# The causal mask of an attention kernel moved from TensorE into the row-maximum instruction, and 128-column products paired

## The chip, the cores and the metric

The kernel runs on one core of one Trainium2 chip. A core has a matrix engine (TensorE, PE in the profile; its weight loads are shown apart as PEld), a vector engine (VectorE, DVE), an engine for functions of one operand (ScalarE, ACT), a general one (GpSimd, POOL) and DMA queues that several engines issue (SP, ACT, POOL). Each engine works through its own list of instructions in order; semaphores order the engines among each other. Operands lie in SBUF, and matmul results in PSUM. Columns stand for the elements along the free dimension, of which each of the 128 partitions has a row.

The metric is the device time of one execution in microseconds (us). Lower is better.

## What is computed

One layer of a decoder, for 512 tokens of width 1024, in float32. The input is normalised, one projection feeds a gated linear attention with four heads and a multi-head latent attention (MLA) with eight heads, both are projected back and merged by gates, and after a residual and a second normalisation comes a squared-ReLU MLP of width 4096. The part that the change touches is the causal softmax of the MLA:

```python
for blk in range(seq // Q_BLOCK):                     # four blocks of 128 queries
    q0, q1 = blk * Q_BLOCK, (blk + 1) * Q_BLOCK
    s = (jnp.einsum('bhqd,bhkd->bhqk', q_nope[:, :, q0:q1], k_nope[:, :, :q1])
         + jnp.einsum('bhqr,bkr->bhqk', q_rope[:, :, q0:q1], k_rope[:, :q1]))
    s = s.astype(jnp.float32) * scale
    mask = (q0 + jnp.arange(Q_BLOCK))[:, None] >= jnp.arange(q1)[None, :]
    p = jax.nn.softmax(jnp.where(mask, s, -jnp.inf), axis=-1).astype(v.dtype)
    outs.append(jnp.einsum('bhqk,bhkv->bhqv', p, v[:, :, :q1]))
```

A block of queries reads the keys up to its own end, so the blocks have 128, 256, 384 and 512 keys, and only the last 128 of each need a mask.

## The kernel before

Matmuls run in a float32 format of reduced precision. To keep float32 accuracy, each operand is split into a high part (rounded, by ScalarE) and a low part (the difference, by VectorE), and a product is the sum of three matmuls: high by high, high by low, low by high. For the weights `pump` does this split (lines 189 and 190) some steps ahead of their use; for activations `split` does (lines 111, 112, 114 and 115). The generic projections are `gemm_fm` (matmuls on lines 245 to 247) and `gemm_tm` (279 to 281).

Work beside the main stream of projections is written as generators. A projection calls `tick` after each of its steps, which lets the first few waiting generators go on to their next `yield`. This gives the order in which instructions are handed to the framework; the framework is asked to plan each engine's order itself (`schedule_with_timeline_sim=True`), so an engine's list follows that plan. `tc.issue_after` puts single instructions behind another one on their engine. Within an engine the order is fixed when the program is built.

The MLA works on pairs of heads. `mla_pair` (line 953) projects queries, keys and values of two heads and starts two generators `mla_head` (line 973), the second some steps after the first. A head goes through four tiles of 128 queries. For tile i with n = 128 (i + 1) keys, a PSUM bank from the pool `px` (four banks, shared with other work) takes:

- three matmuls for the part without positions (lines 984 to 986): high queries by high keys, high by low, low by high;
- two matmuls for the rotary part (lines 987 and 988). Its stationary operand holds the high and the low part of the query on its 128 rows together;
- one matmul of an identity by a mask in bfloat16 (line 989), 0 where a key may be seen and -1e30 where not, onto the last 128 columns.

VectorE then takes the negative of the row maximum from PSUM (991), ScalarE the exponential with that as its bias, from PSUM to SBUF, and the row sum at the same time (994). VectorE inverts the sum (995) and scales the row (996). Once a head's four tiles are there, PE transposes them (1008), they are split, and three matmuls for each block of keys multiply them by the values (1027 to 1029). Then follows the output projection `y_mla`, which `omT` feeds.

Tiles 0 and 2 of a head share one SBUF buffer, `P02`: columns 0 to 127 for tile 0 and 128 to 511 for tile 2. The others come from the pool `B` with 22 buffers.

The constants come with a packed array. `cb` (lines 471 to 474) holds gains, biases, the mask (`neg`) and the rotary frequencies; `identb` (470) and `negb` (491) are its bfloat16 copies that the mask matmul reads. ScalarE's queue issues the DMAs of these constants.

Of the kernel before, what the change touches and what calls it, by code (L numbers as in the profile page):

```python
# [22 lines left out]
NT = T // P  # L23
NK = D // P
LN_EPS = 1e-5
RMS_EPS = 1e-6
GH = 4
# [21 lines left out]
PACK_B = 3 + 2 + NK + GH + 2 * NK + 2 * NK + P + 32  # L49
# [3 lines left out]
def tile_hybrid_block(ctx: ExitStack, tc: tile.TileContext, I, out, dbg=None):  # L53
    nc = tc.nc
    dbg = dbg or {}
    consts = ctx.enter_context(tc.tile_pool(name="consts", bufs=1))
# [9 lines left out]
    def nm(s):  # L66
        uid[0] += 1
        return f"{s}_{uid[0]}"
# [8 lines left out]
    def B(shape, dt=F32, n="b"):  # L77
        return pb.tile(shape, dt, tag="B", name=nm(n))
# [11 lines left out]
    def PX(shape=(P, T), dt=F32, n="px"):  # L90
        return px.tile(list(shape), dt, tag="px", name=nm(n))
# [4 lines left out]
    act = nc.scalar.activation  # L96
# [4 lines left out]
    mm = nc.tensor.matmul  # L101
# [27 lines left out]
    ident = ca[:, 0:P]  # L129
# [2 lines left out]
    mhalf = consts.tile([P, 8], F32, name="mhalf")  # L132
    nc.vector.memset(mhalf, -0.5)
    identr = consts.tile([P, P], F32R, name="identr")
    identb = consts.tile([P, P], BF, name="identb")
    negb = consts.tile([P, P], BF, name="negb")


    stream = []
# [327 lines left out]


    act(identr, ident, AF.Copy)
    act(identb, ident, AF.Copy)  # L470
    cb = consts.tile([P, PACK_B], F32, name="cb")
    nc.scalar.dma_start(cb, I["c_pack_b"])
    cut = np.cumsum([0, 3, 2, NK, GH, 2 * NK, NK, NK, P, 32]).tolist()
    qag, kvg, glg, bga, bgt, ln1g, ln1b, neg, invf = [cb[:, cut[i]:cut[i + 1]] for i in range(9)]
    posi = consts.tile([P, NT], I32, name="posi")
    nc.scalar.dma_start(posi, I["positions"].rearrange("(t p) -> p t", p=P))
    lmask = consts.tile([P, len(LEVELS), 64], U8, name="lmask")
# [1 line left out]
    nc.scalar.dma_start(lmi, I["c_lmask"])  # L479
    wa2 = B([80, T], F32, "wa2")  # L480
    nc.gpsimd.memset(wa2, 0.0)
    for i in range(3):
        nc.scalar.dma_start(wa2[32 * i:32 * i + 16, :], I["w_gla_a2"])
    hbg = consts.tile([P, 2 * NK], F32, name="hbg")
# [3 lines left out]
    def prep():  # L488
        with tc.issue_after(last_in.ins):
            vts(hbg, bgt, 0.5, None, op0=ALU.mult)  # L490
            nc.vector.tensor_copy(negb, neg)
            nc.vector.tensor_copy(lmask, lmi)
        posf = consts.tile([P, NT], F32, name="posf")
        with tc.issue_after(last_in.ins):
            nc.vector.tensor_copy(posf, posi)
        ang = B([P, NT, 32], F32, "ang")
        for tt in range(NT):
            vts(ang[:, tt, :], invf, posf[:, tt:tt + 1], None, op0=ALU.mult)
        yield
        angs = []  # L500
        for sh in (0.0, 0.25):
            kq = B([P, NT, 32], F32, "kq")
            vts(kq, ang, 1.0 / (2.0 * math.pi), sh, op0=ALU.mult, op1=ALU.add)
            vts(kq, kq, MAGIC, None, op0=ALU.add)
            vts(kq, kq, MAGIC, None, op0=ALU.subtract)
            r = B([P, NT, 32], F32, "rr")
            stt(r, kq, -TWO_PI_1, ang, op0=ALU.mult, op1=ALU.add)
            stt(r, kq, -TWO_PI_2, r, op0=ALU.mult, op1=ALU.add)
            stt(r, kq, -TWO_PI_3, r, op0=ALU.mult, op1=ALU.add)
            vts(r, r, sh * 2.0 * math.pi, PI_F, op0=ALU.add, op1=ALU.min)  # L510
            vts(r, r, -PI_F, None, op0=ALU.max)
            angs.append(r)
            yield
        act(sn2[:, :, 32:], angs[0], AF.Sin)
        act(cs2[:, :, :32], angs[1], AF.Sin)
        nc.vector.tensor_copy(cs2[:, :, 32:], cs2[:, :, :32])
        vts(sn2[:, :, :32], sn2[:, :, 32:], -1.0, None, op0=ALU.mult)
        yield
# [403 lines left out]
    scale = HQ ** -0.5  # L922
# [50 lines left out]
    def mla_head(h, hl, qn, kn, vt):  # L973
        for _ in range((0 if h == MH - 1 else STAG) * hl):
            yield
        KK, qs = KKs[0], QS[h]
        Ps = []
        P02 = B([P, T], F32, "P02")
        for i in range(NT):
            n = P * (i + 1)  # L980
            c = slice(i * P, (i + 1) * P)
            p = PX()
            o = p[:, :n]
            mm(o, qn[:, 0, c], kn[:, 0, :n], start=True, stop=False)
            mm(o, qn[:, 0, c], kn[:, 1, :n], start=False, stop=False)
            mm(o, qn[:, 1, c], kn[:, 0, :n], start=False, stop=False)
            mm(o, qs[:, c], KK[:, 0, :n], start=False, stop=False)
            mm(o, qs[:, c], KK[:, 1, :n], start=False, stop=False)
            mm(p[:, c], identb, negb, start=False, stop=True)
            mx = S([P, 1], F32, "mx")  # L990
            nc.vector.tensor_reduce(mx, p[:, :n], axis=AX.X, op=ALU.max, negate=True)
            Pm = P02[:, :P] if i == 0 else P02[:, P:] if i == 2 else B([P, T], F32, "Pm")
            sme = S([P, 1], F32, "sme")
            act(Pm[:, :n], p[:, :n], AF.Exp, bias=mx, accum_out=sme)
            nc.vector.reciprocal(sme, sme)
            vts(Pm[:, :n], Pm[:, :n], sme, None, op0=ALU.mult)
            Ps.append(Pm)
            if i != 0:
                yield

        PT = [A([P, 2, T], F32R, "PT0"), A([P, 2, T], F32R, "PT1"), B([P, 2, 256], F32R, "PT2")]
        plan_t = ([(i, 0, i) for i in range(4)], [(i - 1, 1, i) for i in range(1, 4)] + [(3, 3, 3)],
                  [(i - 2, 2, i) for i in range(2, 4)])
        for b, (pl, pt) in enumerate(zip(plan_t, PT)):
            n = len(pl) * P
            p = PX()
            for cc, j, i in pl:
                nc.tensor.transpose(p[:, cc * P:(cc + 1) * P], Ps[i][:, j * P:(j + 1) * P], ident)
            split(p[:, :n], pt[:, 0, :], pt[:, 1, :])
            if b != 1:  # L1010
                yield
        PT0, PT1, PT2 = PT
        while vt[NT - 1] is None:
            yield
        o = PX()
        for j in range(NT):
            c = slice(hl * P, (hl + 1) * P)
            vh, vl = vt[j][:, 0, c], vt[j][:, 1, c]
            if j == 0:
                ph, pl, od = PT0[:, 0, :], PT0[:, 1, :], o  # L1020
            elif j == 1:
                ph, pl, od = PT1[:, 0, :384], PT1[:, 1, :384], o[:, 128:]
            elif j == 2:
                ph, pl, od = PT2[:, 0, :], PT2[:, 1, :], o[:, 256:]
            else:
                ph, pl, od = PT1[:, 0, 384:], PT1[:, 1, 384:], o[:, 384:]
            mm(od, vh, ph, start=j == 0, stop=False)
            mm(od, vh, pl, start=False, stop=False)
            mm(od, vl, ph, start=False, stop=j == NT - 1)
        yield  # L1030
        om = A([P, 2, T], F32R, "omT")
        st["om"] = split(o, om[:, 0, :], om[:, 1, :])
        omT[h] = om
# [613 lines left out]
```

## Time and profile before

| | before |
|---|---|
| median of three runs | 887.67 us (886.94 to 888.92) |
| profiled execution, first to last instruction (its span) | 884.5 us |
| what lies around the span, against the median | 3.2 us |
| TensorE busy | 868.1 us, 98% |
| weight loads busy | 760.3 us, 86% |
| VectorE busy | 638.4 us, 72% |
| ScalarE busy | 473.6 us, 54% |
| first and last start of a score matmul of line 984 | 344.6 and 453.5 us |

The profile gives one figure for its execution, the span; the time of that very execution as the runs measure it is not listed, so its distance to the median is the best that can be said.

How to read the rows that follow. A row of the timeline has the start (us), the duration (us), the engine, the line of the kernel, the operation, what it writes `<-` what it reads by the program's names, and the shape of the output and of one input; `128*128` ahead of a matmul's shape is the part of the array in use; `x2` means that two instructions in a row are shown as one; a bracket at the end shows how long the engine was idle before, and what ended that. A row of the groups has, after the count, the busy time (us), the mean duration of one instruction (ns), then the idle time before them (us) and what ended it. Matmuls overlap each other, so the distance between their starts tells what one of them costs. The chain that ended last follows the run back from its last instruction, at each step to what released it.

### The profile page before, as it was taken

What the parts mean: (1) busy time and instruction counts of PE and PEld (TensorE: products, weight loads), DVE (VectorE), ACT (ScalarE), POOL (GpSimd) and SP (SyncE); (2) the same over time, 40 slices, a digit from 0 to 9 for tenths busy, and PEclk for the clock granted to TensorE, in tenths of its full rate; (3) what the DMA queues carried; (4) which work ended last, traced back from release to release, by engine and by line L of the source; (5) the groups of instructions that cost most, each with busy time, mean ns of one, the idle gap of its engine ahead of it and who ended that gap; (6) DMA issues with size and microseconds to landing.
All of it is one profiled execution on the core that took longest, in us unless ns stands there. A gap on an engine that the chain in (4) does not pass through costs nothing.

```text
span 884.5 us, 13143 instructions
## 1 busy us (share of the span) xinstructions
PE 868.1 (98%) x4916; PEld 760.3 (86%) x4916; DVE 638.4 (72%) x1019; ACT 473.6 (54%) x834; POOL 185.7 (21%) x200
## 2 busy tenths in 40 slices
PE   6999999999999999999999999999999999999996
PEld 5988888889999988888888888988888888889985
DVE  7859879959665646646866797887557646788865
ACT  6556676556475534435654414566357546656820
POOL 1314457854201010100000003004400520141000
PEclk9999999999999999999999999999999999999999
DMA  7995936795737423112307528006941990399312
GB/s 247 283 221 152 324 110 162 229 215 168 215 87 194 144 78 102 54 54 63 99 19 268 191 72 285 1 1 167 291 113 29 261 254 28 85 232 231 121 61 81
DMA packets 91023, 132.50 MB, mean 150 GB/s; under 512 B 8992, under 2 KB 54432, under 8 KB 90960
## 3 DMA queue, kind: packets, MB, share of 16 engines
q1 hardware_dynamic: 70672, 92.36, 32.5%
q0 software_dynamic: 18368, 35.66, 18.8%
q10 hardware_dynamic: 1920, 3.66, 1.2%
q8 instruction: 38, 0.62, 0.3%
q14 instruction: 25, 0.20, 0.1%
HBM read 110.15 MB, written 8.91 MB: 135 GB/s over the span
## 4 chain that ended last, share of the span: by engine, by line
PE 98%; DMA 1%; ACT 0%; DVE 0%; POOLq 0%; issue 0%; DVEq 0%; ACTq 0%
PE mm L247 11%; PE mm L245 11%; PE mm L246 11%; PE mm L279 6%; PE mm L280 6%; PE mm L281 6%; PE mm L1172 4%; PE mm L1174 4%; PE mm L1173 4%; PE px L1460 2%; PE px L1458 2%; PE px L1459 2%; PE px L849 2%; PE mm L1460 2%; PE mm L1458 2%; PE mm L1459 2%
## 5 line engine op out<-in xcount | busy, mean ns | idle before, releaser
L190 DVE TENSOR_TENSOR wlo<-wraw,whi 128x1024 fp32r<-128x1024 f32 (+1 forms) x90 | 100.1, 1112 | 91.4 <-ACT whi L189 86.6
L189 ACT ACTIVATE whi<-wraw 128x1024 fp32r<-128x1024 f32 (+1 forms) x90 | 85.5, 950 | 81.3 <-PE mm L246 34.7
L246 PE MATMUL mm<-h,whi 128*128 128x512 f32 x224 | 87.2, 389 | 0.0
L245 PE MATMUL mm<-h,whi 128*128 128x512 f32 x224 | 87.1, 390 | 0.0
L247 PE MATMUL mm<-h,wlo 128*128 128x512 f32 x224 | 83.2, 390 | 0.0
L190 DVE TENSOR_TENSOR wlo<-wq,whi 128x1024 fp32r<-128x1024 f32 x44 | 54.5, 1239 | 30.0 <-ACT whi L189 30.0
L1477 POOL DMA_DIRECT2D res<-ev x42 | 37.4, 1000 | 180.7 <-ACT ev L1475 151.5
L189 ACT ACTIVATE whi<-wq 128x1024 fp32r<-128x1024 f32 x44 | 46.5, 1057 | 27.1 <-PE mm L1173 19.0
L1173 PE MATMUL mm<-sh,whi 128*128 128x256 f32 x176 | 49.9, 283 | 0.0
L1172 PE MATMUL mm<-sh,whi 128*128 128x256 f32 x176 | 49.9, 283 | 0.0
L1174 PE MATMUL mm<-sh,wlo 128*128 128x256 f32 x176 | 49.8, 283 | 0.0
L247 PEld LDWEIGHTS mm<-h,wlo 128*128 128x128 f32 x224 | 42.0, 188 | 9.1 <-DVE wlo L190 0.4
L246 PEld LDWEIGHTS mm<-h,whi 128*128 128x128 f32 x224 | 42.0, 188 | 8.8
L245 PEld LDWEIGHTS mm<-h,whi 128*128 128x128 f32 x224 | 42.0, 188 | 8.6
L189 ACT ACTIVATE xh<-wraw 128x1024 fp32r<-128x1024 f32 (+1 forms) x28 | 27.5, 987 | 28.0 <-PE mm L281 15.8
L429 POOL TENSOR_TENSOR mv<-mv,mhalf 128x1 f32<-128x1 f32 x4 | 3.3, 837 | 170.4 <-DVE mv L428 170.4
L190 DVE TENSOR_TENSOR xl<-wraw,xh 128x1024 fp32r<-128x1024 f32 (+1 forms) x28 | 31.3, 1129 | 8.7 <-ACT xh L189 8.7
L793 ACT ACTIVATE E<-rp 128x256 f32<-128x256 f32 x64 | 25.8, 418 | 20.5 <-POOL rp L788 13.7
L1520 ACT ACTIVATE relu<-mm 128x512 f32<-128x512 f32 x24 | 14.1, 596 | 42.0 <-PE mm L247 42.0
L788 POOL TENSOR_TENSOR rp<-rp 128x256 f32<-128x256 f32 x32 | 33.0, 1030 | 9.8 <-ACT q L818 6.1
L787 POOL TENSOR_TENSOR rp<-rp 128x256 f32<-128x256 f32 x32 | 29.6, 926 | 25.3 <-ACT E L793 18.1
L1174 PEld LDWEIGHTS mm<-sh,wlo 128*128 128x128 f32 x176 | 33.8, 192 | 0.0
(472 smaller groups left out, 2821.4 us busy)
## 6 DMA issues: line engine op xcount, KB each, us to landing
wraw<-in_w_ff_dram SPq DMA_DIRECT2D x36, 512.0 KB, 4.8
wraw<-in_w_in_dram SPq DMA_DIRECT2D x30, 512.0 KB, 4.7
wq<-in_w_ff_dram POOLq DMA_DIRECT2D x26, 512.0 KB, 9.4
res<-ev POOLq DMA_DIRECT2D x42, 256.0 KB, 9.4
wq<-in_w_in_dram SPq DMA_DIRECT2D x20, 512.0 KB, 6.6
wq<-in_w_in_dram POOLq DMA_DIRECT2D x18, 512.0 KB, 9.9
hsd<-hs SPq DMA_DIRECT2D x16, 256.0 KB, 3.8
xr<-hsd SPq DMA_DIRECT2D x16, 256.0 KB, 3.7
```

The costliest lines, as they stand in the source:

```text
L189: st["ins"] = act(hi[:, :nk, :n], raw[:, :nk, :n], AF.Copy)
L190: st["lo"] = vtt(lo[:, :nk, :n], raw[:, :nk, :n], f(hi[:, :nk, :n]), op=ALU.subtract)
L245: mm(o, hi[:, c], xh, start=first, stop=False)
L246: mm(o, hi[:, c], xl, start=False, stop=False)
L247: mm(o, lo[:, c], xh, start=False, stop=last)
L279: mm(o, xh, hi[:, :n], start=opens, stop=False, skip_group_check=share)
L280: mm(o, xh, lo[:, :n], start=False, stop=False, skip_group_check=share)
L281: mm(o, xl, hi[:, :n], start=False, stop=last, skip_group_check=share)
L1172: mm(oa, hi[:, k, c], xh, start=opens and k == 0 and a == 0, stop=False, skip_group_check=True)
L1173: mm(oa, hi[:, k, c], xl, start=False, stop=False, skip_group_check=True)
L1174: mm(oa, lo[:, k, c], xh, start=False, stop=k == 3, skip_group_check=True)
L1477: nc.gpsimd.dma_start(res[tt + t][:, j * T:(j + 1) * T], e, accum_op=ALU.add)
```

## The change

The mask matmul goes, and with it the two bfloat16 constants. The mask becomes a float32 tile `masks` of 512 columns, zeros in the first 384 (a memset on GpSimd) and the mask itself in the last 128, so that its last n columns are the mask of a tile with n keys. The packed constants are loaded in three DMAs in place of one, the middle one straight into `masks`.

The row maximum is taken by one instruction on VectorE with two operands, scores and mask. It writes minus their sum to SBUF, and the minimum of that over the row, which is minus the maximum, to `mx`. The exponential then reads this SBUF row with a scale of -1, in place, and no longer PSUM.

The first tile of a head, with 128 keys, gets its five products in three matmuls: the products with the high and the low part of the keys stand side by side as one matmul of 256 columns (two runs of 128 in SBUF), and a further reduction on VectorE adds both halves, from PSUM into the part of `P02` that tile 2 uses later.

```diff
-    identb = consts.tile([P, P], BF, name="identb")
-    negb = consts.tile([P, P], BF, name="negb")
+    masks = consts.tile([P, T], F32, name="masks")
...
-    act(identb, ident, AF.Copy)
-    cb = consts.tile([P, PACK_B], F32, name="cb")
-    nc.scalar.dma_start(cb, I["c_pack_b"])
+    cb = consts.tile([P, PACK_B - P], F32, name="cb")
+    n0 = PACK_B - P - 32
+    for dst, c0, n in ((cb[:, :n0], 0, n0), (masks[:, T - P:], n0, P), (cb[:, n0:], n0 + P, 32)):
+        nc.scalar.dma_start(dst, I["c_pack_b"][:, c0:c0 + n])
...
     nc.gpsimd.memset(wa2, 0.0)
+    nc.gpsimd.memset(masks[:, :T - P], 0.0)
...
-            nc.vector.tensor_copy(negb, neg)
...
-            mm(o, qn[:, 0, c], kn[:, 0, :n], start=True, stop=False)
-            mm(o, qn[:, 0, c], kn[:, 1, :n], start=False, stop=False)
-            mm(o, qn[:, 1, c], kn[:, 0, :n], start=False, stop=False)
-            mm(o, qs[:, c], KK[:, 0, :n], start=False, stop=False)
-            mm(o, qs[:, c], KK[:, 1, :n], start=False, stop=False)
-            mm(p[:, c], identb, negb, start=False, stop=True)
+            if i == 0:
+                w = p[:, :2 * P].rearrange("p (two k) -> p two k", two=2)
+                mm(w, qn[:, 0, c], kn[:, :, :P], start=True, stop=False, skip_group_check=True)
+                mm(o, qn[:, 1, c], kn[:, 0, :P], start=False, stop=False, skip_group_check=True)
+                mm(w, qs[:, c], KK[:, :, :P], start=False, stop=True, skip_group_check=True)
+                s0 = P02[:, P:2 * P]
+                nc.vector.tensor_reduce(s0, p[:, :2 * P].rearrange("p (two k) -> p k two", two=2), axis=AX.X, op=ALU.add)
+                o = s0
+            else:
+                mm(o, qn[:, 0, c], kn[:, 0, :n], start=True, stop=False)
+                mm(o, qn[:, 0, c], kn[:, 1, :n], start=False, stop=False)
+                mm(o, qn[:, 1, c], kn[:, 0, :n], start=False, stop=False)
+                mm(o, qs[:, c], KK[:, 0, :n], start=False, stop=False)
+                mm(o, qs[:, c], KK[:, 1, :n], start=False, stop=True)
+            Pm = P02[:, :P] if i == 0 else P02[:, P:] if i == 2 else B([P, T], F32, "Pm")
             mx = S([P, 1], F32, "mx")
-            nc.vector.tensor_reduce(mx, p[:, :n], axis=AX.X, op=ALU.max, negate=True)
-            Pm = P02[:, :P] if i == 0 else P02[:, P:] if i == 2 else B([P, T], F32, "Pm")
+            nc.vector.tensor_tensor_reduce(Pm[:, :n], o, masks[:, T - n:], scale=-1.0, scalar=3e38,
+                                           op0=ALU.add, op1=ALU.min, accum_out=mx)
             sme = S([P, 1], F32, "sme")
-            act(Pm[:, :n], p[:, :n], AF.Exp, bias=mx, accum_out=sme)
+            act(Pm[:, :n], Pm[:, :n], AF.Exp, scale=-1.0, bias=mx, accum_out=sme)
```

More of the change, by code (lines that the diff above doesn't have):

```diff
@@ L469, in tile_hybrid_block @@
     act(identr, ident, AF.Copy)
-    act(identb, ident, AF.Copy)
-    cb = consts.tile([P, PACK_B], F32, name="cb")
-    nc.scalar.dma_start(cb, I["c_pack_b"])
-    cut = np.cumsum([0, 3, 2, NK, GH, 2 * NK, NK, NK, P, 32]).tolist()
-    qag, kvg, glg, bga, bgt, ln1g, ln1b, neg, invf = [cb[:, cut[i]:cut[i + 1]] for i in range(9)]
+    cb = consts.tile([P, PACK_B - P], F32, name="cb")
+    n0 = PACK_B - P - 32
+    for dst, c0, n in ((cb[:, :n0], 0, n0), (masks[:, T - P:], n0, P), (cb[:, n0:], n0 + P, 32)):
+        nc.scalar.dma_start(dst, I["c_pack_b"][:, c0:c0 + n])
+    cut = np.cumsum([0, 3, 2, NK, GH, 2 * NK, NK, NK, 32]).tolist()
+    qag, kvg, glg, bga, bgt, ln1g, ln1b, invf = [cb[:, cut[i]:cut[i + 1]] for i in range(8)]
     posi = consts.tile([P, NT], I32, name="posi")
```

## The prediction

> **What bounds the kernel now.** I read the page first: the span, the busy times and the chain of work that ended last.
>
> ```profile
> span 884.5 us, 13143 instructions
> PE 868.1 (98%) x4916; PEld 760.3 (86%) x4916; DVE 638.4 (72%) x1019; ACT 473.6 (54%) x834; POOL 185.7 (21%) x200
> PE 98%; DMA 1%; ACT 0%; DVE 0%; POOLq 0%; issue 0%; DVEq 0%; ACTq 0%
> ```
>
> TensorE is busy 98% of the span and makes 98% of the chain. So a matmul taken out is worth its time, provided that nothing else becomes late. The place that decides is the attention stage, from about 345 to 460 us. The second view is the busy time by stretch; columns: busy PE, weight loads (PEld), VectorE (DVE), ScalarE (ACT), GpSimd (POOL), with instruction counts, then clock and DMA.
>
> ```profile
> 345.00:460.00 115.00, 115.00 (x685) 98.91 (x684) 76.48 (x187) 58.59 (x144) 3.04 (x4) 1.00 0.20 61
> ...
> 420.00:440.00 20.00, 20.00 (x126) 17.46 (x125) 17.30 (x41) 13.67 (x34) 0.00 (x0) 1.00 0.31 99
> 440.00:460.00 20.00, 20.00 (x119) 16.85 (x118) 11.97 (x35) 8.87 (x26) 0.00 (x0) 1.00 0.04 14
> ```
>
> In these 115 us PE has no gap, the clock granted is 1.00, and VectorE, which gets the new work, is busy 76.48 us, so 38.5 are free. The tight stretch is 420 to 440 us: 17.30 of 20.
>
> **Term 1, the mask matmuls.** A busy PE hides overlap (a matmul's duration is longer than its distance to the next), so prices are distances between starts. Third view: the timeline of PE and its weight loads at the first head.
>
> ```profile
> 345.63 0.27 PE L987 MATMUL px<-KK,QS 128*128 128x128 f32 x1
> 345.68 0.19 PEld L988 LDWEIGHTS px<-KK,QS 128*128 128x128 f32 x1
> 345.74 0.28 PE L988 MATMUL px<-KK,QS 128*128 128x128 f32 x1
> 345.85 0.10 PEld L989 LDWEIGHTS <-identb 128*128 128x128 bf16 x1
> 345.85 0.23 PE L989 MATMUL px<-negb,identb 128*128 128x128 bf16 x1
> 345.86 0.20 PEld L985 LDWEIGHTS px<-qn,qn 128*128 128x128 f32 x1
> 345.89 0.37 PE L985 MATMUL px<-qn,qn 128*128 128x256 f32 x1
> 346.10 0.28 PE L986 MATMUL px<-qn,qn 128*128 128x256 f32 x1
> 346.22 0.28 PE L987 MATMUL px<-KK,QS 128*128 128x256 f32 x1
> ...
> 346.46 0.23 PE L989 MATMUL px<-negb,identb 128*128 128x128 bf16 x1
> 346.50 0.42 PE L985 MATMUL px<-qn,qn 128*128 128x384 f32 x1
> 346.75 0.33 PE L986 MATMUL px<-qn,qn 128*128 128x384 f32 x1
> 346.92 0.34 PE L987 MATMUL px<-KK,QS 128*128 128x384 f32 x1
> ```
>
> From L987 to L988 (128 columns) is 0.11 us; between two of 256 columns 0.12 (346.10 to 346.22); of 384 columns 0.17 (346.75 to 346.92). The mask's own step is 0.04 (345.85 to 345.89), but the matmul behind it needs 0.21 in place of 0.12, since its weight load only began at 345.86, behind the mask's. So a mask costs 0.25 - 0.12 = 0.13 in the first place and 0.29 - 0.17 = 0.12 in the second. I take 0.12. There are eight heads of four query tiles:
>
> ```profile
> L989 PE MATMUL px<-negb,identb 128*128 128x128 bf16 x32 | 7.3, 230 | 0.0
> L988 PE MATMUL px<-KK,QS 128*128 128x128 f32 x8 | 2.2, 274 | 0.0
> ```
>
> 32 x 0.12 = 3.84 us off PE. Lower bound: only the step itself goes and the wait for the next weights stays, 32 x 0.04 = 1.3.
>
> **Term 2, the first tile's pairs.** Five matmuls of 128 columns (5 x 0.11 = 0.55) become 256 + 128 + 256 columns, 0.12 + 0.11 + 0.12 = 0.35. That is 0.20 for each of the x8 first tiles, 1.6 us. The moving operand now comes in two runs of 128 columns, a form that this trace does not show; if each run cost a matmul of its own, nothing would be gained. Bounds 0 to 1.6; I take 1.6, since the nearest row is the 256-column one. A loss would need a run to cost more than a whole matmul of the same columns.
>
> PE in all: 3.84 + 1.6 = 5.4 us less.
>
> **What VectorE gets.** The fourth view is the groups by shape, VectorE and then ScalarE.
>
> ```profile
> L991 DVE TENSOR_REDUCE mx<-px 128x1 f32<-128x512 f32 x8 | 5.5, 688 | 3.5 <-PE px L989 3.2
> L991 DVE TENSOR_REDUCE mx<-px 128x1 f32<-128x256 f32 x8 | 3.4, 421 | 1.2 <-PE px L989 1.2
> L991 DVE TENSOR_REDUCE mx<-px 128x1 f32<-128x128 f32 x8 | 2.3, 286 | 1.2 <-PE px L989 1.1
> L112 DVE TENSOR_TENSOR PT<-px,PT 128x512 fp32r<-128x512 f32 x12 | 7.8, 684 | 2.6 <-ACT PT L111 2.6
> L112 DVE TENSOR_TENSOR mv<-mm,mv 128x256 fp32r<-128x256 f32 x16 | 6.4, 415 | 0.0
> L995 DVE RECIPROCAL sme<-sme 128x1 f32<-128x1 f32 x32 | 5.1, 160 | 3.6 <-ACT Pm L994 3.0
> ...
> L994 ACT ACTIVATION_READ_ACCUMULATOR Pm<-px,mx 128x1 f32 x16 | 3.1, 193 | 0.0
> L111 ACT ACTIVATE mv<-mm 128x256 fp32r<-128x256 f32 x16 | 5.6, 380 | 2.5 <-DVE mv L112 2.5
> L189 ACT ACTIVATE whi<-wraw 128x256 fp32r<-128x256 f32 x4 | 1.7, 418 | 5.7 <-PE mm L281 4.4 <-PE mm L246 0.7 <-ACT omT L111 0.6
> ```
>
> The fused add-and-minimum isn't in the trace. Its nearest rows are the two-operand instruction from PSUM and SBUF (415 ns at 256 columns, 684 at 512) against the reduction that it replaces (421, 688): no difference. The minimum may need an instruction of its own to be read out, as the sum on ScalarE does (193 ns). Bounds 0 to 0.19; I take 0.16, the [P,1] instruction of the same engine. The first tile gets a further reduction of 256 columns, 0.42. Per head 4 x 0.16 + 0.42 = 1.06 us, for eight 8.5. Lower end 0.42 per head (readout free; a gain is excluded, since as many columns are passed as before). Upper end: the fused instruction takes two cycles for a column. One column is (688 - 286) / 384 = 1.05 ns, so a head's 1280 columns add 1.34, with 4 x 0.19 and 0.42 in all 2.5 per head, 20 us. Even 20 fit into the 38.5 free. In 420 to 440 us lie two score tiles of each width, two heads' worth (the same view for that stretch alone):
>
> ```profile
> L991 DVE TENSOR_REDUCE mx<-px 128x1 f32<-128x512 f32 x2 | 1.4, 688 | 0.6 <-PE px L989 0.6
> ```
>
> There VectorE comes to 17.30 + 2.1 = 19.4 of 20 as I take it, and to 17.30 + 5.0 = 22.3 at the upper end, 2.3 over.
>
> [...]
>
> **Why that isn't on the path.** The chain of a tile (scores, maximum, exponential, scaling, transposes) grows by the readout, and by 0.04 where the exponential reads SBUF in place of PSUM (418 - 380 ns). Behind it PE's queue, which is in order, holds the transposes and then projections. Fifth view: the timeline where scaled tiles meet the transposes that may read them, at the first head and at the last two.
>
> ```profile
> 352.00 0.49 DVE L996 TENSOR_SCALAR Pm<-Pm,sme 128x512 f32<-128x512 f32 x1
> ...
> 354.65 0.27 PE L1008 MATMUL px<-ca,Pm 128*128 128x128 f32 x1
> ...
> 456.00 0.48 DVE L996 TENSOR_SCALAR Pm<-Pm,sme 128x512 f32<-128x512 f32 x1
> 456.75 0.49 DVE L996 TENSOR_SCALAR Pm<-Pm,sme 128x512 f32<-128x512 f32 x1
> ...
> 457.93 0.27 PE L1008 MATMUL px<-ca,Pm 128*128 128x128 f32 x1
> ```
>
> At the first head the last scaled tile is ready at 352.49 and read at 354.65: 2.2 us to spare. At the end it is 0.7 (457.93 - 457.24) to 1.5 (from 456.48), by which of the two is read first. My 1.06 per head fits the first and about fills the second. The fused instruction also waits for its SBUF target, which the exponential did later; behind it on VectorE stand the low halves of the weights, for which PE waits. The PSUM bank comes free before the exponential in place of after it, but PE has no gap to win there. I put all this at 0.
>
> **The start.** ScalarE's queue issues two more DMAs and drops a copy, GpSimd gets a memset of 384 columns.
>
> ```profile
> 1.18 0.45 ACTq L472 DMA_DIRECT2D cb<-in_c_pack_b_dram  x1
> 7.01 1.24 ACT L433 ACTIVATE x<-x,nmr,mvin 128x1024 f32<-128x1024 f32 x1 [2.37 <-DVE nmr L432]
> 8.60 0.52 POOL L481 MEMSET wa<- 80x512 f32 x1
> 21.35 1.44 POOL L429 TENSOR_TENSOR mvin<-mvin,mhalf 128x1 f32<-128x1 f32 x1 [12.23 <-DVE mvin L428]
> ```
>
> 2 x 0.45 goes into the 2.37 us that ScalarE waits before L433, and some 0.5 of memset into GpSimd's 12.23. If that cover went, 0.9 would be lost. The bytes of cb are the same. I take 0.
>
> **Sum.** 884.5 - 5.4 = 879.1 us of span. The median of the three runs is 887.67, 3.2 above the profiled span; the same difference gives 882.3 us, 0.6% faster. 0.2% of 887.67, 1.8 us, is about what a measurement of this kernel can tell from no change.
>
> **The rivals.**
> *The pairs gain nothing* (term 2 at 0): 887.67 - 3.84 = 883.8. For it: the form is new here. Against it: no row shows a price for a moving operand that isn't in one run.
>
> *A short matmul costs by its columns.* From 256 to 384 columns the distance grows by 0.05, so 128 columns would be 0.06. Then a mask is worth 32 x 0.06 = 1.9, and the pairs 5 x 0.06 - (0.12 + 0.06 + 0.12) = 0: 885.8. Against it stands the 0.11 from L987 to L988. [...]
>
> *VectorE holds PE a little*: 420 to 440 overflows by 2.3, and 0.1 at other places: 887.67 - 5.4 + 2.4 = 884.7.
>
> *VectorE's chain becomes the bound (slower).* One mechanism: in each head the transposes reach the front of PE's queue before the scaled tile. At the upper end a head's chain is 2.5 longer, against 0.7 to 2.2 to spare (mean 1.45): 8 x 1.05 = 8.4 us of waits, 887.67 - 5.4 + 8.4 = 890.7. It decides from 0.68 us of stall per head (5.4 / 8). For it: the small margin at the end. Against it: the 38.5 us that VectorE is idle and PE's stretch without a gap.
>
> *The order eats it.* The framework plans each engine's order anew with other durations, and one or two weights or transposes come late for 5 us in all: 887.7. Against it: the work ahead of 344 us hardly changes.
>
> **How the numbers follow.** My sum 0.58 (between 880.3 and 884.3, 2 either way for the new order), no gain from pairs 0.08, columns 0.05, VectorE a little 0.11, VectorE bound 0.11, order 0.07. Faster by over 0.2% (under 885.9): 0.58 + 0.08 + half of the columns case, 0.03, + most of the fourth, 0.09 = 0.78. Same: 0.02 + 0.02 + 0.07 = 0.11. Slower: 0.11. The range from 880.0 to 888.5 leaves out the slow case and a few hundredths below.
>
> **What would show it.** Right: the distance behind a tile's last score matmul is 0.11 to 0.12 without the extra 0.08; the paired matmuls stand 0.12 apart; PE still fills 345 to 455 without gaps; VectorE is busy some 8 us more there. Wrong: PE idle before L1008 put down to the scaling, or low halves that come late; a fused instruction well over 0.69 us at 512 columns; two-run matmuls 0.2 apart. The forecast is wrong if the stalls on PE in the attention stage come to over 3.6 us.

## The result and the profile after

The changed kernel takes 884.5 us, the median of five runs (883.87 to 885.1), against 887.67 of five runs of the kernel before (886.94 to 889.19). The ratio is 0.9963, with a 95% interval from 0.9951 to 0.9975: 0.37% faster. The forecast was 882.3, so of 5.4 us that were to go, 3.2 went. The range (880.0 to 888.5) held it, and the side it gave the most chance, faster, came.

The page of the changed kernel:

```profile
span 882.7 us, 13091 instructions
PE 863.6 (98%) x4868; PEld 758.9 (86%) x4868; DVE 641.9 (73%) x1058; ACT 472.1 (53%) x833; POOL 185.9 (21%) x201
PE 96%; DMA 2%; DVE 1%; ACT 0%; issue 0%; POOLq 0%; DVEq 0%; ACTq 0%
```

The busy time by stretch, with the columns of the prediction (PE, PEld, DVE, ACT, POOL, clock, DMA):

```profile
345.00:460.00 115.00, 113.36 (x662) 99.82 (x662) 81.06 (x230) 59.85 (x148) 3.06 (x4) 1.00 0.21 62
420.00:440.00 20.00, 18.36 (x110) 16.20 (x110) 17.04 (x51) 12.51 (x32) 0.00 (x0) 1.00 0.33 106
```

PE now has a hole of 1.64 us, and all of it lies in the 20 us that the prediction called tight. VectorE, however, is busy for only 17.04 of these 20 us, less than the 17.30 of before: the hole isn't an overflow. The view of PE's waits from 345 to 460 us (it is empty for the kernel before) has one line; its columns are the total, the count and the longest:

```profile
PE px L1036 <- DVE mx L1000: 1.6, 1, 1.6
```

The timeline around it, PE, VectorE and ScalarE together:

```profile
432.36 1.06 ACT L188 ACTIVATE whi<-wraw 128x1024 fp32r<-128x1024 f32 x1 [0.23 <-ACT Pm L1003]
433.33 1.06 ACT L111 ACTIVATE PT<-px 128x512 fp32r<-128x512 f32 x2
433.36 0.34 PE L997 MATMUL px<-KK,QS 128*128 128x384 f32 x1
433.46 1.23 DVE L189 TENSOR_TENSOR wlo<-wraw,whi 128x1024 fp32r<-128x1024 f32 x1 [0.74 <-ACT whi L188]
434.60 0.55 DVE L1000 CUSTOM_DVE_ANT_0 P<-px,masks 128x384 f32<-128x384 f32 x1
435.07 1.28 DVE L112 TENSOR_TENSOR PT<-px,PT 128x512 fp32r<-128x512 f32 x2
435.30 0.47 PE L1036 MATMUL px<-PT,mv 128*128 128x512 f32 x1 [1.60 <-DVE mx L1000]
```

PE has just finished the scores of the sixth head's third tile (line 997) and wants to multiply the fifth head's transposed weights by the values (1036). The pool `px` has four banks, and all four are taken: three by the transposes of the fifth head, one by these scores. The last to read each of them is VectorE: the fused instruction (1000) the scores, line 112 the transposes. Both stand behind the low half of a weight (189), which itself had to wait for its high half on ScalarE. PE goes on 0.15 us after the fused instruction ends. From start to start it is 1.94 us (433.36 to 435.30) where a 384-column matmul takes 0.17: 1.77 us are lost.

Four rows from the same place in the kernel before, VectorE and the first product:

```profile
433.38 1.29 DVE L112 TENSOR_TENSOR PT<-px,PT 128x512 fp32r<-128x512 f32 x2
435.73 0.47 PE L1027 MATMUL px<-PT,mv 128*128 128x512 f32 x1
436.11 0.55 DVE L991 TENSOR_REDUCE mx<-px 128x1 f32<-128x384 f32 x1
436.58 1.22 DVE L190 TENSOR_TENSOR wlo<-wraw,whi 128x1024 fp32r<-128x1024 f32 x1
```

There the low half of this weight (190) stands behind the transposes' split and behind the maximum. The product starts ahead of the maximum of the last scores, and ahead of their exponential (436.70): it got a bank that the split had freed. In the changed kernel the low half stands ahead of them all. PE's order differs too: before, ten projection matmuls (433.54 to 434.70) stand between the last transposes and these scores. That the low half's place decides is shown by an experiment below, the whole split behind `PT`.

To tell what the change itself saved from what other places took, the attention stage is measured from the first matmul of the stage that projects the latents to the last product with the values. The kernel before:

```profile
307.46 0.40 PE L279 MATMUL mm<-whi,latT 128*128 128x256 f32 x2
471.72 0.27 PE L1029 MATMUL px<-PT,mv 128*128 128x128 f32 x1
```

The changed kernel:

```profile
309.17 0.40 PE L278 MATMUL mm<-whi,latT 128*128 128x256 f32 x2
470.10 0.27 PE L1038 MATMUL px<-PT,mv 128*128 128x128 f32 x1
```

The stage went from 164.26 to 160.93 us, 3.33 less; without the hole of 1.77 it is 5.10 less, against 5.4 forecast. The stage begins 1.71 us later than before, a loss that lies ahead of it. Behind the stage next to nothing changed: from its end to the end of the span it is 412.8 us before and 412.6 after. So in these two executions 5.1 were gained, and 1.8 and 1.7 lost.

The paired matmuls, from the timeline of PE at the first head:

```profile
346.75 0.28 PE L986 MATMUL px<-qn,qn 128*128 128x256 f32 x1
346.88 0.23 PE L987 MATMUL px<-qn,qn 128*128 128x128 f32 x1
346.94 0.34 PE L988 MATMUL px<-KK,QS 128*128 128x256 f32 x1
347.11 0.28 PE L993 MATMUL px<-qn,qn 128*128 128x256 f32 x1
...
347.58 0.28 PE L997 MATMUL px<-KK,QS 128*128 128x256 f32 x1
347.70 0.34 PE L993 MATMUL px<-qn,qn 128*128 128x384 f32 x1
```

The three take 0.36 (346.75 to 347.11; forecast 0.35), and behind the second tile's last matmul the next comes 0.12 later (347.58 to 347.70; 0.25 with the mask). VectorE's groups:

```profile
L1000 DVE CUSTOM_DVE_ANT_0 Pm<-px,masks 128x512 f32<-128x512 f32 x8 | 5.5, 688 | 2.1 <-PE px L997 2.0
L990 DVE TENSOR_REDUCE P<-px 128x128 f32<-128x256 f32 x8 | 3.4, 420 | 3.7 <-PE px L988 3.7
L1000 DVE DVE_READ_ACCUMULATOR2_ANT mx<- 128x1 f32 x32 | 2.7, 85 | 0.0
L1000 DVE CUSTOM_DVE_ANT_0 P<-P,masks 128x128 f32<-128x128 f32 x8 | 2.3, 287 | 0.0
```

The fused instruction costs what the reduction did (688 and 287 ns against 688 and 286). Its read-out has a row of 85 ns, but begins before the end of the fused row (435.07 against 434.60 + 0.55 = 435.15 above), so it takes hardly any time of its own.

### The profile page after: what moved, and what is told of

The parts are those of the page before. It is cut to its first block, busy times and chain, and to the rows that moved or that the text cites. A ratio compares the mean times of both kernels' runs of the same rounds, so it can differ in the third digit from the quotient of the medians.

```text
span 882.7 us, 13091 instructions
## 1 busy us (share of the span) xinstructions
PE 863.6 (98%) x4868; PEld 758.9 (86%) x4868; DVE 641.9 (73%) x1058; ACT 472.1 (53%) x833; POOL 185.9 (21%) x201
## 4 chain that ended last, share of the span: by engine, by line
PE 96%; DMA 2%; DVE 1%; ACT 0%; issue 0%; POOLq 0%; DVEq 0%; ACTq 0%
PE mm L244 11%; PE mm L246 11%; PE mm L245 11%; PE mm L279 6%; PE mm L280 6%; PE mm L278 5%; PE mm L1181 4%; PE mm L1183 4%; PE mm L1182 4%; PE px L1469 2%; PE px L1468 2%; PE px L1467 2%; PE px L849 2%; PE mm L1469 2%; PE mm L1467 2%; PE mm L1468 2%
## 5 line engine op out<-in xcount | busy, mean ns | idle before, releaser
L188 ACT ACTIVATE xh<-wraw 128x1024 fp32r<-128x1024 f32 (+1 forms) x28 | 27.2, 986 | 31.2 <-PE mm L280 15.2
L1182 PEld LDWEIGHTS mm<-sh,whi 128*128 128x128 f32 x176 | 33.8, 192 | 0.0
```

The lines of the kernel that those rows point to most:

```text
L188: st["ins"] = act(hi[:, :nk, :n], raw[:, :nk, :n], AF.Copy)
L1182: mm(oa, hi[:, k, c], xl, start=False, stop=False, skip_group_check=True)
```

## The experiments

Two groups of runs: the first takes the change apart, the second goes after the losses. Each time is compared with runs of the kernel before on the same chip, whose medians were 887.41, 886.89 and 886.70 us in the three sets; ratios are to these.

**The same kernel again.** No edit.

> The changed kernel once more, beside the three runs that follow, on their chip. All theories: 884.5 us against 887.7 before (0.3% less), one stall of about 1.8 us at 433 us before a score matmul of the sixth head, and the first matmul at about 9.7 us where the kernel before had it at 8.3. If the stall is an accident of one execution, it is absent or elsewhere here.

Measured: 885.14 us (883.48 to 885.39), ratio 0.997 [0.9959, 0.9982]. The hole is at the same matmul with the same length (1.77 us), so it belongs to the order and not to an execution. What is lost ahead of the stage varies: the first matmul comes at 9.25 us, and the stage begins at 308.48, 1.02 later than before in place of 1.71. Two places make this up. The last projection of the first stage (`xh` by `h`) comes at 46.40 us before the change, at 47.62 in the first profile of the changed kernel and at 46.39 in the second. So by then the first had lost 1.22 us and the second nothing. The timeline of PE in the first profile shows most of this:

```profile
14.54 0.50 PE L278 MATMUL mm<-xh,h 128*128 128x360 f32 x1
14.84 0.50 PE L279 MATMUL mm<-xl,h 128*128 128x360 f32 x1
...
16.32 0.33 PE L279 MATMUL mm<-xl,h 128*128 128x360 f32 x1
16.48 0.33 PE L278 MATMUL mm<-xh,h 128*128 128x360 f32 x1
```

The same matmuls are 0.30 us apart at first and 0.16 later. That changes at about 15.4 us in the first profile and at about 13.1 in the second, so that the first works some 2 us longer at about half the rate. The granted clock is 1.00 in each microsecond from 12 to 17 us of the first profile; what sets the moment no run shows. The rest is lost near 188 us, where the low half of a weight comes late (in the second profile PE waits 0.60 us for it there).

And the stage took 162.44 us, 1.51 more than in the first profile, with the same order and the same hole. The windows behind the hole show why (columns as above, the clock is the number after POOL's):

```profile
436.00:437.00 1.00, 1.00 (x4) 0.74 (x4) 1.00 (x3) 0.00 (x0) 0.00 (x0) 0.70 0.73 283
437.00:438.00 1.00, 1.00 (x4) 0.86 (x3) 0.92 (x4) 0.00 (x0) 0.00 (x0) 0.50 0.08 23
438.00:439.00 1.00, 1.00 (x5) 1.00 (x5) 0.40 (x2) 0.56 (x1) 0.00 (x0) 0.50 0.00 0
439.00:440.00 1.00, 1.00 (x4) 0.76 (x4) 0.65 (x2) 0.25 (x2) 0.00 (x0) 0.60 0.00 0
440.00:441.00 1.00, 1.00 (x6) 0.83 (x5) 0.00 (x0) 0.00 (x0) 0.00 (x0) 1.00 0.00 0
```

Some 2 us after the hole TensorE's granted clock falls to 0.50. By the first four rows (0.70, 0.50, 0.50, 0.60) it stays there for 3.4 us. In the first profile of the same kernel it stays at 1.00.

**The mask alone.** The fused instruction without the pairs:

```diff
-            if i == 0:
-                ... (the three paired matmuls and the reduction on line 990)
-            else:
-                mm(o, qn[:, 0, c], kn[:, 0, :n], start=True, stop=False)
-                ...
+            mm(o, qn[:, 0, c], kn[:, 0, :n], start=True, stop=False)
+            ...
```

> The fused mask instruction without the pairs: the first query tile's scores are five matmuls of 128 columns again, and its extra reduction on VectorE is gone. My terms: against the changed kernel 1.6 us more matmul, so 32 x 0.12 = 3.8 us of TensorE saved against before. The start is the changed kernel's (0.6 to 1.7 us lost). With no new stall 884.5 to 885.5; with a stall like that of the changed kernel, 1.8, 886.3 to 887.3. Rival (a mask is worth its own step alone, 1.3): 887 to 888.

Measured: 890.11 us (884.28 to 893.44), ratio 1.0031 [1.0014, 1.0048]: slower than before, outside all that was expected. The attention stage, however, does what the term said:

```profile
308.14 0.40 PE L278 MATMUL mm<-whi,latT 128*128 128x256 f32 x2
468.78 0.27 PE L1029 MATMUL px<-PT,mv 128*128 128x128 f32 x1
```

It takes 160.64 us, 3.62 less than before, with no hole. So 32 masks are worth 3.6 us (forecast 3.84; the bound that a mask is worth its own step alone, 1.3, is out). The loss comes later. PE's waits from 300 to 560 us:

```profile
PE px L443 <- ACT lnt L448: 3.9, 1, 3.9
```

ScalarE's row at that place:

```profile
539.48 1.06 ACT L188 ACTIVATE whi<-wraw 128x1024 fp32r<-128x1024 f32 x1 [6.07 <-DMA wraw<-in_w_ff_dram]
```

ScalarE waits 6.07 us for a weight to land, and behind that split, in the same queue, stand the instructions that empty the banks of the second normalisation (lines 446 and 448, at 540.44 and 540.89 us). For the very same weight ScalarE waits 0.54 us in the kernel before, 1.01 and 2.15 in the two profiles of the changed one, and 3.12 in a kernel below (the start's order put back), where PE still has no hole at this place. GpSimd's queue issues eight transfers of 512 KB from 528.88 us on here, 0.33 ahead of this weight's own load (529.21). In the changed kernel they begin 0.86 behind it (530.18 against 529.32). After the hole of 4.1 us (537.20 to 541.50, less the usual 0.23) the clock falls to 0.50 again, for 3.4 us by the rows of 0.58, 0.50, 0.50 and 0.71.

**The pairs alone.** The kernel before with the three paired matmuls and the reduction, and with the mask matmul.

> The pairs without the fused instruction: the mask matmul stays, the first query tile is 256 + 128 + 256 columns and the mask, the extra reduction feeds the old maximum. The start is that of the kernel before. My term: 8 x 0.20 = 1.6 us less, 886.1. Rival (a moving operand in two runs costs two matmuls): 887.7. Rival (columns): 887.7. The distances of the paired matmuls in the trace tell it: 0.12 apart or 0.2.

Measured: 886.32 us (885.68 to 886.94), ratio 0.999 [0.9981, 0.9999], a gain of about 0.6. The stage:

```profile
307.57 0.40 PE L279 MATMUL mm<-whi,latT 128*128 128x256 f32 x2
471.19 0.27 PE L1038 MATMUL px<-PT,mv 128*128 128x128 f32 x1
```

163.62 us, 0.64 less. PE's waits show a hole here too, at 445 us:

```profile
PE px L993 <- DVE PT L112: 0.7, 1, 0.7
```

By the starts (444.91 to 445.81, less 0.04) it costs 0.86, so the pairs are worth 1.50 without it (forecast 1.6), and both terms together 5.12, which is the changed kernel's 5.10. The rival that a two-run operand costs two matmuls falls.

**The three DMAs alone.** The kernel before with its constants loaded as in the change.

> The kernel before with nothing but its packed constants loaded by three DMAs in place of one. Theory start: the planned order at the start becomes that of the changed kernel, the first matmul comes at about 9.7 us in place of 8.3, and the time rises by 0.6 to 1.4 us, to 888.3 to 889.1. My prediction's term (two DMAs are hidden): 887.7, and the first matmul at 8.3.

Measured: 887.33 us (886.72 to 889.03), ratio 1.0005 [0.9996, 1.0013]. The planned order at the start is the changed kernel's, ScalarE splits the first weight ahead of the normalisation, and the first matmul comes later, as expected:

```profile
7.68 0.80 ACT L190 ACTIVATE xh<-wraw 128x720 fp32r<-128x720 f32 x1 [3.11 <-DMA wraw<-in_w_in_dram]
...
9.67 1.11 PE L445 MATMUL px<-ca,x 128*128 128x128 f32 x4 [9.67 <-ACT x L434]
```

But the time rises by 0.4 us with an interval that holds zero, less than the 0.6 to 1.4 expected. In this profile too the 360-column projections reach 0.16 us apart only after 15.4 us, and the last of them comes at 47.50, 1.10 later than before.

**The start's order put back.** In the changed kernel the second `bn_stats` of the second input tile is planned behind the first tile's `nmr`:

```diff
+            with ExitStack() as gates:
+                if j == 1 and st.get("nmr"):
+                    gates.enter_context(tc.issue_after(st.pop("nmr").ins))
                 nc.vector.bn_stats(bst[:, j, :], src[:, j * T:(j + 1) * T])
...
-            stt(nmr, mv[:, 0:1], -1.0, mv[:, 1:2], op0=ALU.mult, op1=ALU.mult)
+            st["nmr"] = stt(nmr, mv[:, 0:1], -1.0, mv[:, 1:2], op0=ALU.mult, op1=ALU.mult)
```

> The changed kernel with the second statistics instruction of the second input tile planned behind the first tile's scale-and-shift instruction on VectorE, so that ScalarE normalises before it splits the first weight, as in the kernel before. Theory start: the first matmul comes at about 8.3 us in place of 9.7, the last projection of the latent part at 46.4 in place of 47.6, and the time falls by 0.6 to 1.4 us, to 883.1 to 883.9. Rival DMA: the first matmul waits for the constants that come in more DMAs; then it stays at 9.7 and the time at 884.5.

Measured: 885.86 us (884.18 to 886.86), ratio 0.9979 [0.9969, 0.9988]. The first matmul moved to 9.04 us only, and the last projection of the first stage came at 48.84, later than the 47.62 of the changed kernel's first profile. PE has new waits there, of 0.60 us at 13.36 and 0.63 at 31.09. My theory of the start falls: this order doesn't win the time back.

**One low half behind the fused instruction.**

```diff
+                if st["spl"] == PL["ym", 0]["idx"][1]:
+                    gates.enter_context(tc.issue_after(st["fz"].ins))
                 st["lo"] = vtt(lo[:, :nk, :n], raw[:, :nk, :n], f(hi[:, :nk, :n]), op=ALU.subtract)
...
-            nc.vector.tensor_tensor_reduce(Pm[:, :n], o, masks[:, T - n:], scale=-1.0, scalar=3e38,
+            fz = nc.vector.tensor_tensor_reduce(Pm[:, :n], o, masks[:, T - n:], scale=-1.0, scalar=3e38,
...
+            if h == 5 and i == 2:
+                st["fz"] = fz
```

> The changed kernel with one weight's low half planned behind the fused instruction of the sixth head's third query tile on VectorE; two pairs of matmuls that use that weight swap places, nothing else moves. Theory bank: TensorE's stall at 433 us is the wait for a score bank that the fused instruction frees, and that stood behind this low half. Then the stall goes and the time falls by about 1.8 us, to 882.7. Rival weight: the low half itself is what is wanted; delayed by 0.55 us it makes its own reader wait, and the stall moves by a few us and stays 1 to 2 us long: 884.5. Rival noise: the stall comes from a DMA, and stays where it is.

Measured: 884.79 us (883.35 to 891.15), ratio 0.9972 [0.9958, 0.9987]; no gain. The timeline of PE:

```profile
431.94 0.34 PE L999 MATMUL px<-KK,QS 128*128 128x384 f32 x1
433.03 0.47 PE L1040 MATMUL px<-PT,mv 128*128 128x512 f32 x1 [0.75 <-ACT PT L111]
434.68 0.50 PE L1041 MATMUL px<-PT,mv 128*128 128x512 f32 x1 [1.17 <-DVE PT L112]
```

The first product now starts at 433.03, again 0.15 us after the end of the fused instruction (432.88) and just behind the high half of `PT` (432.97), which the row names. But the second needs the low half of `PT`, which is still behind the weight. Holes of 0.92 and 1.42 us stand in place of 1.77. The bank was only part of the cause: what stands ahead of both readers in VectorE's queue is the whole.

**Both orders.** The two edits above at once.

> Both orders at once. If both theories (bank, start) hold and the gains add, 1.8 + 0.6 to 1.4 us less than the changed kernel: 881.3 to 882.1 us, which is 5.6 to 6.4 less than before, and no gap of more than 0.5 us on TensorE from 300 to 470 us. If the time of the start is taken back by a later wait, 882.7.

Measured: 885.92 us (884.18 to 886.95), ratio 0.998 [0.9971, 0.9988]; the holes are 0.91 and 1.42 us. The first matmul is at 8.47 us, nearly as before the change (8.31), and yet the last projection of the first stage comes at 47.86 (before 46.40). Neither edit helps.

**More work for VectorE.** A second reduction of every score tile, for which the exponential has to wait:

```diff
+            nc.vector.tensor_reduce(S([P, 1], F32, "mx2"), Pm[:, :n], axis=AX.X, op=ALU.max)
             sme = S([P, 1], F32, "sme")
```

> The changed kernel with a second reduction behind each fused instruction on VectorE, which the exponential has to wait for: 4 reductions per head, 0.29 + 0.42 + 0.55 + 0.69 = 1.95 us, 15.6 us on VectorE in all, to 97 of the 115 us of the attention stage. Theory covered: VectorE's time is hidden but for single places such as the stall at 433 us; 884.5 to 888. Rival (VectorE's chain is the bound): the 0.7 to 2.2 us to spare at each head's transposes are used up, and a good part of 15.6 us shows: 892 to 900.

Measured: 886.08 us (884.83 to 887.82), ratio 0.9991 [0.9983, 1.0]. The same stretch as above:

```profile
345.00:460.00 115.00, 112.42 (x649) 98.43 (x648) 89.99 (x260) 59.67 (x145) 3.00 (x4) 1.00 0.20 61
```

VectorE is busy 8.9 us more there than in the changed kernel, and PE 0.94 less. The rows of the 32 reductions add to 15.2 us (15.6 expected), but they overlap the rows around them, so VectorE's busy time over the whole span rises by 9.5 us only. Four holes of 0.40 to 1.55 us add to 3.4; without them the stage is again 5.0 shorter than before. So VectorE's sum isn't the bound, as I had it, and single places in its queue are.

**The whole split behind PT.** In the changed kernel both halves of that weight are planned behind the split of the fifth head's transposes:

```diff
-            act(hi, src, AF.Copy)
+            st["hi"] = act(hi, src, AF.Copy)
...
+                late = st["spl"] == PL["ym", 0]["idx"][1]
+                if late:
+                    gates.enter_context(tc.issue_after(st["pt"][0].ins))
                 st["ins"] = act(hi[:, :nk, :n], raw[:, :nk, :n], AF.Copy)
+                if late:
+                    gates.enter_context(tc.issue_after(st["pt"][1].ins))
                 st["lo"] = vtt(lo[:, :nk, :n], raw[:, :nk, :n], f(hi[:, :nk, :n]), op=ALU.subtract)
...
-            split(p[:, :n], pt[:, 0, :], pt[:, 1, :])
+            s1 = split(p[:, :n], pt[:, 0, :], pt[:, 1, :])
+            if h == 4 and b == 1:
+                st["pt"] = (st["hi"], s1)
```

> The changed kernel with the split of the weight at 433 us (ScalarE's high half and VectorE's low half) planned behind the split of the transposed weights PT of the fifth head. Theory banks: the stall of 1.8 us is the wait for one of the four score banks, all in use by the transposes and the last scores, because their readers on VectorE (the fused instruction and the PT split) stand behind a weight's low half. With both readers ahead of it the gap at the first product of the fifth head falls from 1.8 to under 0.5 us, and the time by 1.3 to 1.8, to 882.7 to 883.7. Rival order: any new order brings a stall of 1 to 4 us of its own somewhere; then 884 to 887.

Measured: 883.56 us (882.39 to 883.8), ratio 0.9957 [0.9945, 0.997]. PE's waits:

```profile
PE px L998 <- DVE P L995: 0.5, 1, 0.5
...
PE px L1043 <- DVE PT L112: 0.2, 1, 0.2
```

The hole at the products shrank to 0.37 us (432.05 to 432.60, less the usual). A new one of 0.73 stands at 442.5, where the first tile's reduction is late. The stage is 160.16 us (307.92 to 468.08), 4.10 less than before, the shortest of all.

**GpSimd's transfers held, mask alone.** In the mask-only kernel a copy of one column waits for the late weight, and GpSimd's transfers stand behind it:

```diff
+        gates = ExitStack()
+        if ci == 0:
+            e = stream[PL["f1", 0, 4]["idx"][1]]
+            g = nc.gpsimd.tensor_copy(S([P, 1], F32, "hold"), e["raw"][:, 0, :1])
+            gates.enter_context(tc.issue_after(g.ins))
         for op, i, j in (("12", 0, 1), ("11", 0, 0), ("22", 1, 1), ("21", 1, 0)):
...
+        gates.close()
```

> The mask-only kernel with one instruction more on GpSimd, a copy of one column that waits for the late weight to land, and the eight 512 KB transfers of GpSimd's queue behind it. Theory collision: the 4 us stall at 537 us of the mask-only kernel comes from these eight transfers, which start beside the weight's last half megabyte and slow it; then the weight lands by 534, the stall goes, and the time falls from 890.1 to 883.5 to 885 (before, less 3.6 for the mask matmuls, with 0 to 1 for the start). Rival: the weight is late for another reason (issued late, a buffer): then the stall stays and the time at 889 to 891.

Measured: 884.43 us (883.45 to 884.92), ratio 0.9968 [0.9956, 0.9981], where the same kernel without the hold stood at 1.0031. ScalarE's timeline:

```profile
533.42 1.06 ACT L188 ACTIVATE whi<-wraw 128x1024 fp32r<-128x1024 f32 x1 [0.71 <-DMA wraw<-in_w_ff_dram]
```

From its issue to its split the weight needs 4.8 us (528.63 to 533.42) in place of 10.3 (529.21 to 539.48). The hole is gone, and the order of all other instructions on PE, VectorE and ScalarE is the same: the collision of the two queues was the cause. The mask part alone is thus worth 0.32% once nothing collides.

**Both remedies, and the hold alone.** The changed kernel with the split behind PT and the hold, and with the hold alone.

> The changed kernel with both edits, the split behind PT and GpSimd's transfers behind the weight. If both theories hold, no gap over 0.8 us on TensorE between 300 and 560 us, no fall of the clock ahead of the end, and the whole 5.1 us that the attention stage saved without its stall, less 0 to 1 at the start: 882.0 to 883.3. Rival order: 884 or more.

> The changed kernel with GpSimd's eight transfers held behind the weight alone. In the changed kernel the weight landed in time (ScalarE waited 1.0 and 2.2 us for it in its two profiles and TensorE not at all), so the median hardly moves, 884.0 to 885.0, and the slow executions go: the highest under 886. Rival: the transfers that now start later make the sums of the second stage late, 886 or more.

Measured: 883.17 us (882.65 to 884.22), ratio 0.9959 [0.9946, 0.9973], with both; 883.83 us (883.16 to 886.19), ratio 0.9969 [0.9958, 0.9981], with the hold alone. Both remedies give the lowest median of all, 3.5 us under before. Its interval overlaps that of the changed kernel (0.9951 to 0.9975), so that it beats it isn't shown by the times; the smaller holes are shown by the traces (with both, none between 300 and 560 us is above 0.73 us, and the clock doesn't fall there). The highest run with the hold alone was 886.19, a little above what I expected.

## Why the prediction was right or wrong

The time, 884.5 us, lies in the wide range but not in the 880.3 to 884.3 that the sum was given. The saving was right; what was lost elsewhere had been put at nothing.

**Term 1, the masks, right.** 3.84 forecast; 3.62 and 3.60 in the two mask-only profiles (308.10 to 468.76 in the second).

**Term 2, the pairs, right.** 1.6 forecast, 1.50 measured. The two runs of the operand cost nothing that can be seen. The rivals "the pairs gain nothing" and "a short matmul costs by its columns" are out by the sum. The single distances are 0.13, 0.06 and 0.17 us, not 0.12, 0.11 and 0.12 as I had them: the 128 columns between the pairs do step by 0.06, as the second rival said, and the next pair pays it back. (That rival's own step is 0.12 - 0.05 = 0.07 and not 0.06, which would have made its masks 2.2 us, its pairs 0.3 and its time 885.1.)

**VectorE's prices, right or better.** The fused instruction costs what I took: 688 ns at 512 columns from PSUM and SBUF, and 287 at 128 columns with both sources in SBUF, where the reduction took 688 and 286. The two cycles for a column, from which the upper end and the sums of two rivals came, were a supposition that no run shows. The read-out is an instruction of its own, 32 of them. Its row is 0.085 us where I took 0.16, and nearly all of it lies under the fused row (at one place it runs from 435.07 to 435.15, where the fused row ends), so that the bound "readout free" was the true one. Over the whole span VectorE is busy 3.5 us more (638.4 to 641.9), which the eight new reductions explain, 8 x 0.42 = 3.4. In 345 to 460 us it is 4.6, not 8; some 1 us of that is other work that the new order moved into the stretch.

**"I put all this at 0", wrong.** This is the step that failed. I had compared the margins at the transposes, seen that banks come free earlier, and named the low halves that stand behind the fused instruction. The trace shows the other direction: the fused instruction and the split of `PT` stand behind a low half, PE wants a bank, and all four are waiting for VectorE. It isn't the move of the bank's release from ScalarE to VectorE that costs: before, the exponential that freed the scores' bank had to wait for the maximum on VectorE anyway (0.57 us, to 436.70). The mask-only kernel moves the release in the same way and has no hole; its order has this low half (435.31) behind the split of `PT` (432.10), as in the kernel before. The pairs alone leave the release of three tiles in four on ScalarE and have a hole of 0.86. What costs is the new order, with a weight's low half ahead of the readers of all four banks. That one place cost 1.77 us, and the split put behind `PT` brought it to 0.37.

**The rival "VectorE holds PE a little"** had the stretch (420 to 440 us), nearly the size (2.4 us) and the time (884.7) of what came, at a chance of 0.11. Its mechanism was wrong: I priced it by the sum of the busy time, 22.3 of 20 us, and VectorE was idle for 3 of those 20. What it needed was to ask which instruction stands ahead of which. **"The order eats it"**, 0.07, was underrated, and its mechanism is the one that came: of the kernels with the fused instruction or the pairs only the mask-only one, without and with the hold, had no hole in the attention stage, and without the hold it ran into a transfer, whose 4.1 us ate more than the whole gain. **"VectorE's chain becomes the bound"** is out: with 8.9 us more on VectorE the ratio rose by 0.002 to 0.003, some 2 us.

**The start, "I take 0", a little wrong.** The stage of attention began at 307.46 in the kernel before and at 307.57 with the pairs alone; in the twelve profiles with three DMAs it began between 307.75 and 309.67. That is 0.3 to 2.2 late. Putting the order of the first instructions back didn't help (two runs), and the DMAs alone cost 0.4 us with an interval from -0.4 to 1.2. In the first profile most of it is the later moment from which the matmuls stand 0.16 us apart in place of 0.30, and the second, of the same kernel, had lost nothing by 46 us; so it belongs in part to the execution. Whether the change moves that moment, and why the weight near 188 us comes late, stays open.

**The sum.** Saved 5.1; lost 1.8 in the hole, some 0.3 to 1.7 ahead of the stage, and 1.5 in those executions where the clock fell behind the hole. Without the clock that leaves 1.6 to 3.0 us; 3.2 and 2.3 were measured. The 3.2 us that I had put around the span are 1.8, by the spans of the runs of the changed kernel (884.5 us with a span of 882.7); the rest was the profiled execution of before being 1.4 under its median. As I used only a difference, that did no harm.

## What to carry to other kernels

On a bound engine, price what is taken off by the distance between starts; that held within 0.3 of 5.4 us here. Then ask of each buffer that the bound engine waits for what stands ahead of its last reader in that reader's queue, and how many other buffers of that pool wait for the same queue. Here neither VectorE's busy share (17.04 of 20 us) nor the engine that releases a bank told it; the planned order did. Where a framework plans the order anew, give that a loss of a few us rather than zero, and look for transfers that were landing just in time: the burst on GpSimd's queue began 1.30 us earlier in the mask-only kernel than in the changed one (528.88 against 530.18), and ScalarE waited 6.07 us in place of 1.01 for the last piece on another queue.

## What the runs showed of the hardware

A hole on TensorE cost more than its length in some executions here. In the second profile of the changed kernel the clock fell to 0.50 for 3.4 us behind a wait of 1.6 us, and the stage grew by 1.51 us; in the first, with the same wait, it stayed at 1.00. In the mask-only kernel it fell to 0.50 for 3.4 us behind the hole of 4.1. What sets off the fall no run shows. The mean clock over an execution was 0.996 or less in none of 74 runs of the kernel before, in 5 of 12 of the changed kernel, in 10 of 12 of the mask-only one with its hole of 4.1 us, and in none of 15 of the three kernels whose holes were mended. It was so in 7 of 16 runs of the two other kernels that kept the hole of 1.77 us (the start's order put back, the hold alone) and in 12 of 24 with the holes of 0.9 and 1.4 us, but in none of 11 with the second reduction, whose longest hole is 1.55 us. The two profiles of the changed kernel have a mean clock of 0.998 without the fall and 0.996 with it. By that, the medians of the kernels with such holes mix executions with and without a fall.

Eight transfers of 512 KB on one queue slowed half a megabyte on another so much that it needed 10.3 us from its issue to its use, against 4.8 where they were held back until it had landed; ScalarE waited 6.07 us for it, against 0.71. They began 0.33 us ahead of the weight's issue in the kernel with 10.3 us, and 0.86 behind it in the changed kernel with 5.1 (529.32 to 534.41).
